# Moving places, splits and first loads around the low weights of a split-float32 encoder kernel

## The chip, the core and the metric

The kernel runs on one core of one Trainium2 chip. The metric is the device time of one execution in microseconds, lower is better. The engines are named as the profile names them: PE (TensorE, matmuls), PEld (its weight loads, which overlap the matmuls), DVE (VectorE), ACT (ScalarE), POOL (GpSimd) and SP (SyncE, which here issues most DMAs; SPq in a row is its queue).

## What is computed

One layer of a streaming encoder on 1024 prompt frames and 64 sample frames (1088 rows), all in float32: an input projection, a gated convolution, chunk-band attention, a gated merge, an output projection, and a SwiGLU feed-forward of width 2816.

```python
proj = xn @ w_in                    # cb, cc, ch, q, k, v, ga, gb
cv, conv_state = causal_conv(cc * ch, conv_prefix, w_conv)
ya = (cb * cv) @ w_conv_out
o, new_k, new_v = attn_fn(heads(q), heads(k), heads(v))
yb = o.reshape(B, L, ATT_DIM) @ w_attn_out
merged = jax.nn.sigmoid(ga) * ya + jax.nn.sigmoid(gb) * yb
x = x + merged @ w_out
x = x + (jax.nn.silu(xn2 @ w1) * (xn2 @ w3)) @ w2      # xn2 = rmsnorm(x)
return rmsnorm(x, g_final), conv_state, new_k, new_v
```

## The kernel before

**Split products.** A float32 operand is split in two float32r parts: ACT casts the high part, DVE subtracts it from the source to get the low part (`split`, lines 126 to 130). A product is then three matmuls, high by high, low rows by high weights, and high rows by low weights.

**Units.** The big projections go in units of 256 weight columns, 1024 deep, against all 1088 rows. A unit does seven block products (`STEPS`, a Strassen form of a 2 by 2 block product), each of 24 matmuls of 128x272. `Unit.prep(step)` makes the weights of one product; `run` issues a unit's products and, after each, calls `prep` of the next unit (`ahead`, a list of units and of the steps to be done at each turn). There are twelve units of the input projection (q, k and so on), then gates, attention, the merge, the output projection `wo`, and 22 units of the feed-forward's way up, named a0, b0, a1 ... b10 (a: `w_ff1`, b: `w_ff3`). The way down follows, in four blocks of two or three pairs of h columns, each block in two halves (g) of seven products.

**Places of the low weights.** High weights live in `ws`, eight buffers that rotate. Low weights live in one tile, `low`, in eight places of 512 columns: `slots` adds one to `taken` and takes the place `taken % 8`. Users put a shift on top: 0 for units, 40 for the merge's weights, 24 for `wo` (where the part in `low` is the high one), and 8 for the down products' h tiles (`h_load`, lines 1374 to 1390, which puts every second h tile in `ws` and the others in `low`). A shifted use of a place therefore reaches into the first columns of the next place; the framework that places the semaphores sees such an overlap and orders the two uses.

**First loads of the way down.** `refill` issues h loads as long as `held` plus the next group stays within 16 tiles; a group of the first block has two tiles. `held` starts at 14, so the first call (line 1527, before the last unit's products) loads group 0; `Refill.prep`, called after each product of b10, takes 2 off and loads the next group. SP issues DMAs in its program's order and waits there for each one's semaphores.

**Order.** The framework lists each engine's instructions by its own plan; `tc.issue_after(x)` pins what is issued within it behind instruction x. In `ahead` the entry `{2: (0, 1, 2)}` of the third unit makes steps 0, 1 and 2 after product 2, but after product 1 it falls back on step 1 as well, so that step 1 is split twice, in the projection's third unit (k0) and in the feed-forward's (a1).

**k tiles.** In the projections, small tiles share one scratch tile, `scr`, by lists of places: `KF` for a k result of 544 columns, `CC` and `STAGE` for others, with overlaps between them. The attention cache's tiles (`cache_tile`) use `CC`, in the order 4896, 5988, 9264, and are stored by DMA before a place can be used again.

Of the kernel before, what the change touches and what calls it, by code (L numbers as in the profile page):

```python
# [66 lines left out]
def encoder_kernel(ctx: ExitStack, tc: tile.TileContext, ins, outs):  # L67
# [49 lines left out]
    def table_load(j, t):  # L117

        t = tables[j] = t.rearrange("p (h n) -> p h n", h=2)
        src = ins["bias_ext"][2 * j, 384:]  # L120
        nc.sync.dma_start(t, bass.AP(tensor=src.tensor, offset=src.offset, ap=[[0, P], [768, 2], [1, 384]]))

    def table_store(j):
        nc.sync.dma_start(bias_d[2 * j : 2 * j + 2].rearrange("h (p n) -> p h n", n=384), tables.pop(j))
# [17 lines left out]
    taken = [-1]  # L142
# [55 lines left out]
    def temp():  # L198
        temps[0] += 1
        return temps[1][:, temps[0] % 2]  # L200

    class Unit:
        def __init__(self, src, nm):
            self.nm = nm
            self.raw = rpool.tile([P, KD, 2 * P], F32, tag="raw", name=f"raw{nm}")
            nc.sync.dma_start(self.raw, src.rearrange("(k p) n -> p k n", p=P))
            self.w = {}
# [8 lines left out]
        def prep(self, step):  # L216

            a11, a12, a21, a22 = self.block(0, 0), self.block(0, 1), self.block(1, 0), self.block(1, 1)

            def sum(o, x, y, op=ALU.subtract):  # L220
                vec.tensor_tensor(o, x, y, op=op)

            if step == 0:
                self.plain(1, a11)
            elif step == 1:
                self.plain(2, a12)
            elif step == 2:
                self.s1 = temp().rearrange("p (k n) -> p k n", k=4)
                sum(self.s1, a21, a22, ALU.add)
                self.s2 = temp().rearrange("p (k n) -> p k n", k=4)  # L230
                sum(self.s2, self.s1, a11)
                self.plain(6, self.s2)
            elif step == 3:
                sum(a21, a11, a21)
                self.plain(7, a21)
            elif step == 4:
                self.plain(5, self.s1)
            elif step == 5:
                self.plain(4, a22)
            else:  # L240
                sum(a12, a12, self.s2)
                self.plain(3, a12)

    newest = [None, None]
# [49 lines left out]
    def plain_load(i):  # L294
        ld, kt, at = plan[i]
        if "raw" not in ld:
            raw = rpool.tile([P, kt, ld["w"]], F32, tag="raw", name=f"rawp{i}")
            nc.sync.dma_start(raw, ld["src"].rearrange("(k p) n -> p k n", p=P))
            ld["raw"] = raw
# [58 lines left out]
    X, GM, SUMS, KEPT, VST, SQ, FEW = (0, 1024, 9264), 2048, 3072, (4096, 5120), (6144, 7168), 8192, 9216  # L358
    V32 = [10288]
    SNAP, STAGE, CC, UT = [544 * i for i in range(4)], [2720, 3808, 9264], [4896, 5988], [7080, 8172]  # L360
    KF = [*CC, 2176]
    turn = {tuple(KF): 0}

    def slot(places, n):

        k = turn[tuple(places)] = turn.get(tuple(places), -1) + 1
        a = places[k % len(places)]
        return scr[:, a : a + n]
# [164 lines left out]
    def unit_of(n):  # L533
        nm, u, src = units[n]
        return Unit(src, f"{nm}{u}")
# [35 lines left out]
    def whole(t, src, snap):  # L571

        two = t.rearrange("p (j n) -> p j n", j=2)
        if snap is None:
            act.copy(two, src)
        else:
            vec.tensor_tensor(two, src, snap, op=ALU.add)
# [53 lines left out]
    def k_done(u):  # L631
        def f(r, h, src, snap):
            kf = slot(KF, HT)
            whole(kf, src, snap)
            st = stage()
            split(st[:, 0], st[:, 1], kf)
            to_heads(k_d, st, 2 * u + r, h)
            late.append(lambda: k_out(2 * u + r, h, kf))
# [76 lines left out]
    def cache_load(i):  # L715
        cts[i] = ct = slot(UT, 2 * ATT)
        nc.gpsimd.dma_start(ct[:, :ATT], ck[i * P : (i + 1) * P])
        nc.gpsimd.dma_start(ct[:, ATT:], cvv[i * P : (i + 1) * P])

    def cache_tile(i):  # L720
        ct = cts[i]
        with tc.issue_after(newest[1]):
            put_v(slot(CC, 2 * ATT), ct[:, ATT:], P, TP + i * P, nc.sync)
        pk = bank1("BD", f"ckp{i}")[:, 0]
        for hp in range(4):
            nc.tensor.transpose(pk[:, hp * P : (hp + 1) * P], ct[:, hp * P : (hp + 1) * P], ident)
        st = slot(CC, 2 * ATT).bitcast(F32R).rearrange("p (l a t) -> p l a t", l=2, a=4)
        split(st[:, 0], st[:, 1], pk.rearrange("p (a t) -> p a t", a=4))
        dst = k_d[:, :, :, T + i * P : T + (i + 1) * P].rearrange("(a j) d l t -> (j d) l a t", j=2)
        for l in range(2):  # L730
            nc.sync.dma_start(dst[:, l], st[:, l].bitcast(F32))
# [9 lines left out]
    def run1(n, unit, ahead):  # L741
        nm, u, _ = units[n]
        return run(unit, x7, bank1, snap1, DONE[nm](u), ahead)
# [4 lines left out]
    ahead = []  # L748
# [7 lines left out]
    for n in range(len(units)):  # L756
        if n in (5, 6):
            for j in range(2):
                table_store(2 * (n - 5) + j)
        if n in (4, 5):  # L760
            for j in range(2):
                table_load(2 * (n - 4) + j, slot(STAGE, 768))
        if n == 0:
            r, si = r0, 2
        else:
            if n + 1 < len(units):
                nxt_unit = unit_of(n + 1)
                new = [(nxt_unit, {2: (0, 1, 2)} if n == 1 else {})]
            else:
                new = [(PlainNext(), {})]  # L770
                plain_load(0)
            if n == 1:
                ahead += new
                r, si = r1, 2
            else:
                r, si = run1(n, unit, new), 0
            unit = nxt_unit
        for _ in r:
            if n < 2 and si in (2 + n, 5 + n):
                i = 2 * n + si // 5  # L780
                cache_tile(i)
                if i + 2 < 4:
                    cache_load(i + 2)
            if si > 1:
                for f in due:
                    f()
                due.clear()
            due += late
            late.clear()
            si += 1  # L790
# [326 lines left out]
    def wo_half(hf):  # L1117
        r = []
        for kq in range(2):
            raw = rpool.tile([P, 4, 512], F32, tag="raw", name=f"wor{hf}_{kq}")  # L1120
            nc.sync.dma_start(
                raw,
                ins["w_out"][0][kq * 512 : (kq + 1) * 512, hf * 512 : (hf + 1) * 512].rearrange(
                    "(k p) n -> p k n", p=P
                ),
            )
            for k in range(4):
                hi, lo = moving_pair(f"o{hf}_{kq}_{k}")
                split(hi, lo, raw[:, k])
                r.append((hi, lo))  # L1130
        return r
# [34 lines left out]
    if True:  # L1166
# [2 lines left out]
        act.activation(gb_row, gb_row, AF.Copy, scale=-0.5)  # L1169

        two_sums = early.tile([P, 2, D], F32, tag="raw", name="two_sums")
        w = wo_half(0)
        for i in ORDER:
            t0, n = TT[i]
# [214 lines left out]
            ht.append(t)  # L1389
        hts.append(ht)  # L1390

    held = [14]

    def refill():

        while len(hts) < len(loads_h) and held[0] + len(loads_h[len(hts)][0]) <= 16:
            held[0] += len(loads_h[len(hts)][0])
            h_load(*loads_h[len(hts)])

    class Refill:  # L1400
        def prep(self, step):
            held[0] -= 2
            refill()

    class Down:
# [73 lines left out]
    def up_unit(n):  # L1479
        l, p = names[n]  # L1480
        return Unit(ins["w_ff1" if l == "a" else "w_ff3"][0][:, 2 * p * P : 2 * (p + 1) * P], f"{l}{p}")
# [3 lines left out]
        return run(unit, operands, bank2, snap2, (gate_done if l == "a" else hidden_done)(p), ahead)  # L1485


    u0, u1 = up_unit(0), up_unit(1)
    u0.prep(0)
    u0.prep(1)  # L1490
# [28 lines left out]
    for n in range(1, len(names)):  # L1519
        if n + 1 < len(names):  # L1520
            unit = up_unit(n + 1)
            ahead = [(unit, {2: (0, 1, 2)} if n == 1 else {})]
        else:
            for kp in (*blocks[0], blocks[1][0]):
                W2[kp] = Down(kp)
            ahead = [(W2[kp], {}) for kp in blocks[0]] + [(Refill(), {})]
            refill()
        if n in (4, 6):
            nm, src = (("k", ck), ("v", cvv))[n // 2 - 2]
            with tc.issue_after(stored[0]):  # L1530
                nc.gpsimd.dma_start(outs[f"cache_{nm}_sample"][: CACHE - TS], src[TS:])
        if n == 1:
            nxt += ahead
            r = r1
        else:
            r = up_run(n, this, ahead)
        for _ in r:
            for f in kept_now:
                f()
            kept_now[:] = last_keep  # L1540
            last_keep.clear()
        this = unit
# [173 lines left out]
```

## Time and profile before

| what | value |
|---|---|
| time, median of 3 runs | 1515.86 us (1514.68 to 1515.95) |
| the profiled execution | 1516.27 us, span of the profile 1514.2 us |
| PE busy | 1475.1 us, 97% of the span |
| DVE busy | 981.1 us, 65% |
| ACT busy | 679.3 us, 45% |
| DMA | 264.72 MB, mean 175 GB/s |

By stretches of the span (us; the bounds are chosen by hand):

| stretch | what runs | PE busy of | granted PE clock |
|---|---|---|---|
| 0 to 70 | norm, v | 66.12 of 70 | 1.00 |
| 70 to 161 | q and k units | 89.86 of 91 | 1.00 |
| 320 to 600 | gates and attention | 278.46 of 280 | 1.00 |
| 645 to 760 | end of the merge, wo | 114.13 of 115 | 1.00 |
| 800 to 860 | up units begin | 58.19 of 60 | 1.00 |
| 860 to 1150 | up units | 289.68 of 290 | 1.00 |
| 1209 to 1275 | last up unit | 46.24 of 66 | 0.74 |
| 1275 to 1325 | way down begins | 50.00 of 50 | 1.00 |
| 1480 to 1514 | end | 26.34 of 34 | 0.93 |

A row of the timeline reads: start, duration, engine, line of the kernel, operation, output and inputs, shapes, count, and in brackets the engine's idle time just before it and what ended it. A row of the table of waits reads: who waited, for whom, then us in total, how many times, and the longest. A row of a table of windows gives the window, its length, each engine's busy time and count, the granted PE clock (1.00 is full), the DMA engines' share and GB/s.

### The profile page before, as it was taken

The page shows a single profiled execution, that of the slowest core. Times are in us where ns is not written, and L with a number is a line of the kernel's source. Part 1 is how long each engine was busy: PE and PEld are TensorE (multiplying, and loading weights), DVE is VectorE, ACT ScalarE, POOL GpSimd, SP SyncE. Part 2 cuts the span into 40 slices and gives each one's busy share as a digit, 9 for nine tenths or more (in the row PEclk, how much of TensorE's full clock was granted, in tenths as well). Part 3 has the DMA queues.
Part 4 walks back from the last instruction along what each step waited for, and adds up shares of the span by engine and source line. Part 5 has one row for each costly group of instructions (what it writes and reads, how often), then busy time and mean ns, then how long its engine had stood idle before and what let it go on. Part 6 is the DMA issues. An engine that isn't in the chain of part 4 may idle for free.

```text
span 1514.2 us, 26487 instructions
## 1 busy us (share of the span) xinstructions
PE 1475.1 (97%) x10200; PEld 1382.5 (91%) x10200; DVE 981.1 (65%) x1852; ACT 679.3 (45%) x1398; POOL 133.1 (9%) x243
## 2 busy tenths in 40 slices
PE   8999999999999999999999999999999967999997
PEld 6899999999989999998888999999999966888886
DVE  7975565725767646661798666667677635857577
ACT  7654333425767635430456444444444423513123
POOL 1400010001111110001000001010111100000000
PEclk9999999999999999999999999999999977999999
DMA  8685623287766468434424444444434434776675
GB/s 285 188 272 195 199 86 115 46 251 215 200 171 177 114 197 285 153 96 144 150 71 159 154 148 157 157 153 147 157 132 154 147 118 164 271 247 229 224 266 202
DMA packets 164029, 264.72 MB, mean 175 GB/s; under 512 B 18624, under 2 KB 98688, under 8 KB 163872
## 3 DMA queue, kind: packets, MB, share of 16 engines
q1 hardware_dynamic: 143040, 196.13, 41.3%
q0 software_dynamic: 19712, 64.81, 11.8%
q10 hardware_dynamic: 1152, 2.10, 0.4%
q8 instruction: 80, 1.31, 0.4%
q14 instruction: 45, 0.37, 0.1%
HBM read 172.89 MB, written 91.92 MB: 175 GB/s over the span
## 4 chain that ended last, share of the span: by engine, by line
PE 70%; issue 16%; DVE 5%; DMA 4%; ACT 2%; POOL 2%; SPq 1%; POOLq 0%; ACTq 0%; DVEq 0%
PE A L1629 8%; PE D L1629 4%; PE Ab L266 4%; PE Aa L266 3%; PE g L330 2%; PE g L331 2%; PE g L332 2%; PE B L1629 2%; PE wo L1139 2%; PE wo L1141 2%; PE wo L1140 2%; PE t L952 2%; PE Db L266 2%; PE pv L977 2%; DMA low<-h_d 2%
## 5 line engine op out<-in xcount | busy, mean ns | idle before, releaser
L330 PE MATMUL g<-xn,wp 128*128 128x272 f32 x384 | 112.7, 293 | 0.0
L331 PE MATMUL g<-xn,wp 128*128 128x272 f32 x384 | 111.6, 291 | 0.0
L332 PE MATMUL g<-xn,low 128*128 128x272 f32 x384 | 110.6, 288 | 0.0
L128 ACT CAST ring<-w2r 128x512 fp32r<-128x512 f32 (+1 forms) x78 | 42.6, 587 | 109.4 <-PE A L1629 50.3
L128 ACT CAST hq<-sa 128x512 fp32r<-128x512 f32 x73 | 45.2, 619 | 82.3 <-DVE sa L1334 54.6
L1318 POOL DMA_DIRECT2D h_d<-hq x73 | 38.9, 533 | 433.5 <-DVE hq L129 234.9
L863 DVE CUSTOM_DVE_ANT_0 p<-s,bb 128x640 f32<-128x640 f32 (+5 forms) x72 | 47.5, 661 | 42.4 <-DMA qd<-q_d 27.1
L330 PEld LDWEIGHTS g<-xn,wp 128*128 128x128 f32 x384 | 72.3, 188 | 0.9
L332 PEld LDWEIGHTS g<-xn,low 128*128 128x128 f32 x384 | 72.3, 188 | 0.5
L331 PEld LDWEIGHTS g<-xn,wp 128*128 128x128 f32 x384 | 72.3, 188 | 0.1
L1629 PE MATMUL A<-ring,low 128*128 128x512 f32 x264 | 72.4, 389 | 0.0
L1629 PE MATMUL A<-ring,ht 128*128 128x512 f32 x264 | 72.2, 389 | 0.0
L129 DVE TENSOR_TENSOR hq<-sa,hq 128x512 fp32r<-128x512 f32 x73 | 50.4, 691 | 29.8 <-ACT hq L128 29.6
L266 PE MATMUL Ab<-tt,wb 128*128 128x272 f32 x352 | 60.9, 296 | 2.7 <-ACT sb_Q L254 2.0
L129 DVE TENSOR_TENSOR low<-rawa,wa 128x512 fp32r<-128x512 f32 x56 | 38.4, 688 | 38.8 <-ACT wa L128 38.8
L129 DVE TENSOR_TENSOR ring<-w2r,ring 128x512 fp32r<-128x512 f32 (+1 forms) x78 | 48.9, 648 | 22.4 <-ACT ring L128 22.4
L266 PE MATMUL Ab<-mg,wb 128*128 128x272 f32 x352 | 60.9, 296 | 0.8 <-DVE sb L1329 0.8
L266 PE MATMUL Aa<-tt,wa 128*128 128x272 f32 x352 | 58.2, 287 | 1.7 <-ACT sa_Q L254 1.6
L1629 PEld LDWEIGHTS A<-ring,low 128*128 128x128 f32 x264 | 49.6, 188 | 10.3
L1629 PEld LDWEIGHTS A<-ring,ht 128*128 128x128 f32 x264 | 49.5, 188 | 10.3
L266 PE MATMUL Aa<-mg,wa 128*128 128x272 f32 x352 | 57.8, 286 | 0.5 <-DVE sa L1299 0.5
L128 ACT CAST wa<-rawa 128x512 fp32r<-128x512 f32 x56 | 34.6, 620 | 51.7 <-PE Ab L266 33.7
(543 smaller groups left out, 4511.9 us busy)
## 6 DMA issues: line engine op xcount, KB each, us to landing
h_d<-hq POOLq DMA_DIRECT2D x73, 512.0 KB, 3.4
ht<-h_d SPq DMA_DIRECT2D x77, 256.0 KB, 3.5
low<-h_d SPq DMA_DIRECT2D x77, 256.0 KB, 3.5
rawa<-in_w_ff SPq DMA_DIRECT2D x11, 1024.0 KB, 5.9
rawb<-in_w_ff SPq DMA_DIRECT2D x11, 1024.0 KB, 5.3
w2r<-in_w_ff SPq DMA_DIRECT2D x11, 1024.0 KB, 7.2
qd<-q_d SPq DMA_DIRECT2D x32, 272.0 KB, 4.5
rawp<-in_w_in SPq DMA_DIRECT2D x6, 1024.0 KB, 6.5
```

The costliest lines, as they stand in the source:

```text
L128: a = act.copy(hi, src)
L129: b = vec.tensor_tensor(lo, src, hi.bitcast(F32), op=ALU.subtract)
L266: newest[0] = mm(t[:, j, :HN], w[:, k, :], x[p][:, k, l, j * HN : (j + 1) * HN], start=p in (1, 2, 7) and k == 0 and n == 0, stop=k == 3 a ...
L330: mm(out, a, first, start=k == 0, stop=False)
L331: mm(out, a, then, start=False, stop=False)
L332: mm(out, b, p, start=False, stop=k == kt - 1)
L863: vec.tensor_tensor_reduce(out=s if len(ps.shape) == 2 else s.rearrange("p (a b) -> p a b", a=2), in0=ps, in1=bias if len(ps.shape) == 2 e ...
L952: nc.tensor.transpose(tp[:, i * P : (i + 1) * P], s[:, i * P : (i + 1) * P], ident)
L977: mm(pv[:, :, lo:hi], v[:, kb, :], pt[:, :, kb - base, lo:hi], start=i == 0, stop=i == len(blocks) - 1,)
L1139: mm(ps, x(k, 0), wh, start=f, stop=False)
L1318: stored[0] = nc.gpsimd.dma_start(h_d[p, c - 1], hq.rearrange("p i l t -> p (i l t)").bitcast(F32)).ins
L1629: mm(t, ht[k][:, j, x], w[:, l], start=p in (1, 2, 7) and k == 0 and n == 0, stop=k == len(ks) - 1 and n == 2, skip_group_check=p in (6, 5 ...
```

## The change

There are five edits. The k tiles' places become 4896, 2176, 5988 in that order, from the first. The third unit's step 1 is split once, in both stages, and in the feed-forward its splits are pinned behind the newest snapshot copy of PE's results on ACT (`newest[1]`). Ahead of `wo` one place of `low` is skipped. The way down's `held` starts at 16, the early call of `refill` is gone, and the last `Refill.prep` takes 4 off instead of 2, so that each group is issued one product later in the program and the last turn issues two.

```diff
-    KF = [*CC, 2176]
-    turn = {tuple(KF): 0}
+    KF = [CC[0], 2176, CC[1]]
+    turn = {}
...
-                new = [(nxt_unit, {2: (0, 1, 2)} if n == 1 else {})]
+                new = [(nxt_unit, {1: (), 2: (0, 1, 2)} if n == 1 else {})]
...
         two_sums = early.tile([P, 2, D], F32, tag="raw", name="two_sums")
+        taken[0] += 1
         w = wo_half(0)
...
-    held = [14]
+    held = [16]
...
     class Refill:
         def prep(self, step):
-            held[0] -= 2
+            held[0] -= 2 if step < 6 else 4
             refill()
...
+    class Behind:
+        def __init__(self, unit):
+            self.unit = unit
+
+        def prep(self, step):
+            with tc.issue_after(newest[1]):
+                self.unit.prep(step)
...
-            ahead = [(unit, {2: (0, 1, 2)} if n == 1 else {})]
+            ahead = [(Behind(unit), {1: (), 2: (0, 1, 2)})] if n == 1 else [(unit, {})]
         else:
...
             ahead = [(W2[kp], {}) for kp in blocks[0]] + [(Refill(), {})]
-            refill()
```

The count of places moves with it. Up to b10 the kernel before takes 8 places for v, 85 for the twelve units (one of them the double split), 40 for the gates and the merge, 16 for `wo` and 148 for 21 up units (again one double): 297, so b10 begins at place 297 mod 8 = 1. The changed kernel takes 8 + 84 + 40 + 1 + 16 + 147 = 296 and b10 begins at place 0. With the shift of 8, group n of the h loads writes, in the kernel before, the columns 512n + 8 to 512n + 520, of which the last eight are the first low weights of b10's product n. In the changed kernel group 0 writes 3592 to 4104, where b10 has nothing, and group n from 1 on writes over product n - 1 and the first eight columns of product n.

PE, the beginning of b10 (Ab, Bb and Db are PSUM tiles of its products, wb_1, wb_2, wb_7 high weights, low the low ones; what an instruction waits for stands in brackets). The kernel before:

```order
L266 MATMUL Ab_13872<-mg_6860,wb_1_13677 128x272 x3
L266 MATMUL Bb_13907<-mg_6861,wb_2_13708 128x272 [waits PE_49]
L266 MATMUL Bb_13907<-mg_6861,wb_2_13708 128x272 x3
L266 MATMUL Db_13984<-tt_8099,wb_7_13770 128x272 [waits DVE_49]
L266 MATMUL Db_13984<-tt_8099,wb_7_13770 128x272 x3
L266 MATMUL Ab_13872<-mg_6860,low 128x272 [waits DMAHW5_49]
L266 MATMUL Ab_13872<-mg_6860,low 128x272
```

The changed kernel, from the same place:

```order
L266 MATMUL Ab_13863<-mg_6857,wb_1_13671 128x272 x3
L266 MATMUL Ab_13863<-mg_6857,low 128x272 x2
L266 MATMUL Ab_13863<-mg_6857,wb_1_13671 128x272 x4
L266 MATMUL Ab_13863<-mg_6857,low 128x272 x2
L266 MATMUL Ab_13863<-mg_6857,wb_1_13671 128x272 x4
```

Before, the first low matmul of each of the seven products waits for a DMA (the load of the h tile that shares eight columns with it), and the high matmuls of the next products were drawn ahead of it. In the change no matmul of b10 waits for a DMA and the products stand one after the other.

ACT, the beginning of the feed-forward (sb_Q is the copy of a PE result that frees the PSUM tile Ab for b0's next product; wa are a1's high weights, cast from the raw weights rawa). The kernel before:

```order
L1303 ACTIVATE sa_10_9209<-sa_10_9209 128x544
L128 CAST wa_2_9247<-rawa_9245 128x512
L128 CAST wa_1_9276<-rawa_9245 128x512
L1297 ACTIVATE sa_01_9239<-Aa_8904 128x544
L128 CAST wa_2_9279<-rawa_9245 128x512
L128 CAST wa_6_9284<-sf_8893 128x512
L254 COPY sb_Q<-Ab_8995 128x544
```

The changed kernel:

```order
L1304 ACTIVATE sa_10_9206<-sa_10_9206 128x544
L1298 ACTIVATE sa_01_9236<-Aa_8901 128x544
L254 COPY sb_Q<-Ab_8992 128x544
L128 CAST wa_1_9270<-rawa_9242 128x512
L128 CAST wa_2_9273<-rawa_9242 128x512
```

Five instructions stood between the activation and sb_Q, four of them casts of a1's weights; now the copy stands ahead of all of a1's casts, of which there is one less.

DVE, the first k result (scr from Bk) in the k unit. The kernel before, then the changed one:

```order
L577 TENSOR_TENSOR scr<-Bk_1270,scr 128x544 [waits DMAHW7_49,DMAHW2_49]
L577 TENSOR_TENSOR scr<-Ak_1241,scr 128x544 [waits PE_49,Activation_49]
L577 TENSOR_TENSOR scr<-Dk_1336,scr 128x544 [waits DMAHW5_49,PE_49]
```

```order
L577 TENSOR_TENSOR scr<-Bk_1267,scr 128x544 [waits DMAHW5_49,PE_49,Activation_49]
L577 TENSOR_TENSOR scr<-Ak_1238,scr 128x544 [waits PE_49,Activation_49]
L577 TENSOR_TENSOR scr<-Dk_1333,scr 128x544 [waits DMAHW7_49,DMAHW2_49,PE_49]
```

The wait for the cache's last two k stores (DMAHW7 and DMAHW2, line 731, which read place 5988) moves from the first k result to the third, and the wait for the cache's last v store (DMAHW5, line 377, which reads place 4896) from the third to the first.

At `wo` the cast of its first high weights moves from a place whose columns overlap those of the merge's last weights to one that doesn't, so six of `wo`'s first eight splits stand ahead of the merge's last instructions on DVE instead of behind them.

## Prediction

> **What bounds the kernel now.** I began with the page: PE is busy for 97% of the span, so time can come only from its idle stretches or from the speed of its matmuls.
>
> ```profile
> span 1514.2 us, 26487 instructions
> PE 1475.1 (97%) x10200; PEld 1382.5 (91%) x10200; DVE 981.1 (65%) x1852; ACT 679.3 (45%) x1398; POOL 133.1 (9%) x243
> PEclk9999999999999999999999999999999977999999
> ```
>
> 39 us are idle, and in slices 33 and 34 of 40 (1211 to 1287 us) the granted clock is not full. The table of waits, for PE alone, says which waits these are:
>
> ```profile
> PE Ab L266 <- DMA low<-h_d: 12.0, 4, 3.4
> PE Db L266 <- DMA low<-h_d: 3.4, 2, 2.3
> PE Ab L266 <- ACT sb_Q L254: 2.0, 2, 1.3
> PE Bb L266 <- DMA low<-h_d: 1.3, 1, 1.3
> PE ktp L624 <- DVE scr L577: 1.1, 1, 1.1
> PE wo L1143 <- ACT low L128: 0.8, 1, 0.8
> ```
>
> Seven waits, 12.0 + 3.4 + 1.3 = 16.7 us, are for the way down's h loads into `low`. All are in the last up unit, b10. The timeline gives its first instruction, its first wait, its last instruction and the way down's first:
>
> ```profile
> 1218.34 0.66 PE L266 MATMUL Ab<-mg,wb 128*128 128x272 f32 x4
> 1223.34 0.82 PE L266 MATMUL Ab<-mg,low 128*128 128x272 f32 x2 [3.33 <-DMA low<-h_d]
> 1274.00 0.41 PE L266 MATMUL Ab<-mg,low 128*128 128x272 f32 x2
> 1274.24 0.85 PE L1629 MATMUL A<-ring,ht 128*128 128x512 f32 x3
> ```
>
> So b10 lasts 1274.24 - 1218.34 = 55.90 us. The table of windows sets it beside an undisturbed unit (first row), parts of b10 that follow a wait, and the way down (last two rows):
>
> ```profile
> 1176.90:1197.62 20.72, 20.72 (x170) 20.72 (x169) 12.65 (x21) 7.93 (x17) 1.06 (x2) 1.00 0.27 96
> 1218.34:1274.24 55.90, 36.19 (x170) 33.29 (x169) 18.31 (x31) 11.73 (x23) 1.59 (x3) 0.69 0.34 119
> 1223.30:1228.50 5.20, 4.90 (x20) 4.58 (x20) 0.20 (x1) 0.22 (x1) 0.00 (x0) 0.50 0.00 0
> 1247.70:1250.60 2.90, 2.75 (x20) 2.53 (x20) 0.00 (x0) 0.06 (x1) 0.00 (x0) 1.00 0.00 0
> 1253.90:1258.80 4.90, 4.90 (x20) 4.58 (x20) 0.00 (x0) 0.00 (x0) 0.00 (x0) 0.50 0.01 3
> 1275.00:1325.00 50.00, 50.00 (x224) 41.48 (x223) 41.15 (x70) 26.87 (x53) 2.67 (x5) 1.00 0.79 276
> 1325.00:1480.00 155.00, 155.00 (x695) 128.67 (x694) 104.06 (x178) 36.54 (x71) 0.00 (x0) 1.00 0.72 241
> ```
>
> The same work takes 20.72 us in a unit and 55.90 in b10. Of the difference, 55.90 - 36.19 = 19.7 us is idle (the seven waits and 3.0 us more for drains), and 36.19 - 20.72 = 15.5 us is matmuls at a low clock: twenty matmuls take 4.90 us at 0.50 and 2.75 at 1.00. From 1275 to 1480 PE never idles: that stage sets its own length, and follows wherever b10 ends.
>
> **Part by part: the low places and the first loads.** By the order, b10's matmuls wait for no DMA any more. What they still wait for are the drains of PSUM on ACT and DVE, as in every unit. If these are in time, b10 takes 20.72 us and ends at 1218.34 + 20.72 = 1239.06: **35.2 us** less. The drains share their engines with the splits for the way down, which had 55.90 us before. Is 20.72 enough? On DVE the first of that work waits for a weight load, and the rate is seen where DVE runs without a gap:
>
> ```profile
> 1216.94 0.37 SPq L1411 DMA_DIRECT2D w2r<-in_w_ff  x1
> 1222.08 0.69 DVE L1426 TENSOR_TENSOR w2r<-w2r 128x512 f32<-128x512 f32 x1 [5.17 <-DMA w2r<-in_w_ff]
> 1278.21 0.69 DVE L1321 TENSOR_TENSOR sa<-sa,sa 128x512 f32<-128x512 f32 x1
> 1278.82 0.69 DVE L129 TENSOR_TENSOR ring<-sa,ring 128x512 fp32r<-128x512 f32 x1
> 1274.93 0.84 PE L1629 MATMUL A<-ring,low 128*128 128x512 f32 x3
> ```
>
> On DVE, start to start is 0.61 us. SP issues that weight load at 1216.94, before b10 begins, so its landing doesn't move. In the changed order 31 DVE instructions go from this one to the product on b10's last PSUM tile that the way down's second product waits for; two of them are short. By 29 x 0.61 + 0.2 = 17.9 us DVE is there at 1240.0 us; PE needs it at 1239.06 plus the first product of 12 matmuls. Three of those start every 0.68 us (1274.93 follows 1274.24 by 0.69), 2.7 us in all, so at 1241.8: 1.8 us to spare. The drain that b10's last product needs (start 1239.06 - 2.96 = 1236.1) is the 20th: 1222.08 + 19 x 0.61 + 0.1 = 1233.8, or right after product 4 at 1233.1 + 0.7; the way down's first product needs the 25th by 1239.06, at 1236.9. ACT has 11.73 us of work in the whole of b10. So I take the full 35.2; should the cover fail, the ends are 19.7 (idle gone, clock not) and 35.2.
>
> The loads themselves: group n is issued when b10's product n has begun to read its low weights, every 2.96 us (a seventh of 20.72) from 1221 on, the last at 1239, and used at 1239 + 2.7n and later. Group 1, issued at 1222, is needed at 1241.8. They land within
>
> ```profile
> DMA to landing us min/median/max: 2.9/4.2/11.3
> w2r<-in_w_ff SPq DMA_DIRECT2D x11, 1024.0 KB, 7.2
> ```
>
> (the second row, the median of the kind of weight load above, is for a rival), so even the longest, 11.3 us, is hidden: 0. The extra SP waits on PE hold only loads that are used later: 0.
>
> **The k tiles.** The first k result waited for the cache's last k store (issued at 116.35), and PE waited for the result:
>
> ```profile
> 117.50 0.41 PE L266 MATMUL Bk<-xn,low 128*128 128x272 f32 x2
> 121.15 0.72 DVE L577 TENSOR_TENSOR scr<-Bk,scr 128x544 f32<-128x544 f32 x1 [2.10 <-DMA k_d<-scr]
> 131.22 0.73 DVE L577 TENSOR_TENSOR scr<-Dk,scr 128x544 f32<-128x544 f32 x1 [0.69 <-PE Dk L266]
> 122.02 0.27 PE L624 MATMUL ktp<-ident,scr 128*32 128x128 f32 x1 [1.14 <-DVE scr L577]
> 111.44 0.36 SPq L377 DMA_DIRECT2D v_d<-scr  x1
> 116.35 1.07 SPq L731 DMA_DIRECT2D k_d<-scr  x1
> 104.65 3.62 DMA v_d<-scr
> ```
>
> Now it waits for the v store of 111.44. An earlier one took 3.62 us, so this is there at 115.1, before the matmuls end (117.9). The result is ready at about 118.7, two microseconds before PE wants it (120.9). The wait for the k store moves to the third result, whose matmuls end at 131.2, ten after the landing at 121.1. **1.1 us** (ends: 0 and 1.1).
>
> **The feed-forward's third unit.** ACT's casts of a1 waited for its raw weights, and the copy that PE needed stood behind them:
>
> ```profile
> 810.61 1.14 ACT L128 CAST wa<-rawa 128x512 fp32r<-128x512 f32 x2 [4.32 <-DMA rawa<-in_w_ff]
> 813.78 0.61 ACT L254 COPY sb_Q<-Ab 128x544 f32<-128x544 f32 x1
> 814.44 0.77 PE L266 MATMUL Ab<-tt,wb 128*128 128x272 f32 x4 [1.34 <-ACT sb_Q L254]
> 809.72 0.41 PE L266 MATMUL Ab<-tt,low 128*128 128x272 f32 x2
> ```
>
> The copy now stands ahead and can start when its matmuls end, at 810.1; PE wants it at 814.44 - 1.34 = 813.1. **1.3 us** (ends 0 and 1.3). Late next would be a1's own splits, but a1 begins only after a further unit has run. The two double splits that go (an ACT cast and a DVE subtraction of the 0.69-us kind each) ran beside PE: 0 further.
>
> **wo.** PE's 0.8 us for the cast ends, since that cast no longer waits for the merge's last matmul.
>
> ```profile
> 671.86 0.29 PE L332 MATMUL yb<-ob,low 128*128 128x272 f32 x1
> 674.19 0.19 DVE L129 TENSOR_TENSOR ms<-ga,ms 128x32 fp32r<-128x32 f32 x1
> ```
>
> In return wo's first tile is not interleaved with the second and needs DVE's last merge rows after 14 matmuls, 3.2 us into it at 0.23 us each (a third of the 0.69 above, the same shape); before, these rows were done 2.3 us after the merge's end (674.38 against 672.15). **0.8 us** (ends 0 and 0.8; a loss would need DVE 0.9 us later).
>
> **Sum.** 35.2 + 1.1 + 1.3 + 0.8 = 38.4 us off the profiled span of 1514.2: 1475.8. That execution took 1516.27, 0.41 above the median of the runs, 1515.86; off the median the forecast is **1477.4 us**.
>
> [...] The row 1223.30:1228.50 shows 0.50 right behind a gap of 3.33 us, and 1253.90:1258.80 too. [...] The trace sides with the gaps as the cause: 20.72-us units at 1.00 stand ahead, and the way down at 1.00 behind.
>
> **Rivals.** *The clock stays low in b10.* If something other than the waits lowers it (both quoted stretches at 0.50 last 5 us, longer than the gap ahead), the idle time goes, the 15.5 us stay: 1477.4 + 15.5 = 1492.9. Against it: it is 1.00 in all other units, with the same matmuls.
>
> *DVE becomes the bound at the end of b10.* If the weight load lands at 7.2 us after issue (the median of its kind on the page) instead of some 5, and DVE paces at 0.69, the 31 instructions end at 1224.1 + 20.2 = 1244.3, 2.5 us late; with a clock drop behind it, up to 5: 1480 to 1482.5. For it: DVE has hardly a gap left there. Against: the way down kept DVE at 41 of 50 us without a PE wait.
>
> *The waits move to the way down: slower.* If the loads, now issued behind the products of a short b10, are not ahead of PE, each product of the way down's first block pays what b10's paid, 35.2 / 7 = 5.0 us. From 8 products on (38.4 / 5.0) the change loses; all fourteen would give 1477.4 + 70 = 1547. Against it: 11.3 us at worst to land, with 17 and more to go, and PE at 50.00 of 50 while the same loads run.
>
> *The change doesn't take the waits away.* Then only the three small terms are left: 1515.86 - 3.2 = 1512.7. The order of the built program speaks against it.
>
> **How the numbers follow.** Forecast 0.83, DVE bound 0.10, clock 0.03, moved waits 0.02, waits kept 0.02. The likeliest gives 1477.4. The range starts 2 us below it, since no more waits than these end, and goes past the DVE case to 1484; outside are about 0.1. What can be told from no change is 0.2%, 3 us: faster 0.97, within 0.01, slower 0.02.
>
> **What would show it.** In the new profile b10 should run about 20.7 us at clock 1.00, without a row of PE waiting for low<-h_d, and the waits for ktp, sb_Q (the longer one) and wo's cast be gone; PE idle falls from 39 to about 16 us. A PE wait at L1637 or L1472 in the first 10 us of the way down would mean the DVE rival. I am wrong if b10 stays above 25 us, or if the way down grows by more than it shrinks.

## The result, and the profile after

| | before | after |
|---|---|---|
| median of four runs | 1515.9 us | 1475.53 us |
| lowest and highest | 1514.68, 1517.61 | 1475.21, 1479.49 |
| span of the profiled execution | 1514.2 us | 1473.8 us |

The ratio of the times is 0.9739, 95% interval 0.9720 to 0.9758: 40 us faster. The forecast was 1477.4. In some executions below, a stretch of the up units or of the way down runs 1.8% slower at a granted clock of 1.00 (321 matmuls instead of 327 in 40 us), so stages are compared there, not whole times.

The head of the changed kernel's page, and of its table of waits for PE the only rows of 0.6 us and more:

```profile
span 1473.8 us, 26481 instructions
PE 1458.0 (99%) x10200; PEld 1369.7 (93%) x10200; DVE 979.2 (66%) x1850; ACT 678.1 (46%) x1396; POOL 133.1 (9%) x243
PEclk9999999999999999999999999999999999999999
```

```profile
PE warm L443 <- ACT ones L441: 2.9, 1, 2.9
PE Aa L266 <- ACT sa_Q L254: 1.3, 1, 1.3
PE pvv L512 <- ACT low L128: 0.9, 1, 0.9
PE xt L1212 <- DVE xg L1201: 0.6, 1, 0.6
```

PE's idle time is 15.8 us instead of 39, the granted clock has no slice of the page below 0.9 left, and no row of PE waits for `low<-h_d`, for `ktp`, for `sb_Q` or at `wo`. Then b10 and the way down in windows (us; busy time of PE, PEld, DVE, ACT and POOL, granted clock, DMA share, GB/s), and the timeline where the one ends and the other begins, with DVE's first and last work for it:

```profile
1213.13:1233.85 20.72, 20.72 (x171) 20.72 (x170) 16.82 (x28) 11.37 (x22) 1.06 (x2) 1.00 0.82 264
1235.00:1285.00 50.00, 50.00 (x224) 41.48 (x223) 41.92 (x72) 26.66 (x52) 3.21 (x6) 1.00 0.81 292
```

```profile
1216.71 0.69 DVE L1427 TENSOR_TENSOR w2r<-w2r 128x512 f32<-128x512 f32 x1 [5.02 <-DMA w2r<-in_w_ff]
1233.85 0.85 PE L1637 MATMUL A<-ring,ht 128*128 128x512 f32 x3
1234.66 0.71 DVE L1328 TENSOR_TENSOR sa<-Ab,sa 128x544 f32<-128x544 f32 x1
1236.57 0.84 PE L1637 MATMUL B<-ring,ht 128*128 128x512 f32 x3
```

b10 takes 20.72 us, an undisturbed unit's time to the hundredth, where it took 55.90. The way down behind it fills its 50.00 us of 50 as before. From its first matmul to the end of the span it is 1473.8 - 1233.85 = 239.95 us, before 1514.2 - 1274.24 = 239.96: nothing is given back later. DVE was done with b10's last tile at 1235.37, and PE came for the tile at 1236.57, so 1.2 us were to spare.

**Where the 40.4 us come from.** Each row compares the start of the same PE instruction in both traces; the change of that lead from row to row is what a place gave.

| place | start before | start after | lead | given there |
|---|---|---|---|---|
| k unit, last product ahead of `ktp` | 117.75 | 117.90 | -0.15 | |
| k unit, behind the first `ktp` | 122.04 | 120.89 | 1.15 | 1.30 |
| k unit, behind the last `ktp` | 148.52 | 147.82 | 0.70 | -0.45 |
| merge (yb) | 587.98 | 587.07 | 0.91 | 0.21 |
| up units, behind `wo` | 796.96 | 794.59 | 2.37 | 1.46 |
| b0, behind `sb_Q` | 817.52 | 813.53 | 3.99 | 1.62 |
| b10 begins | 1218.34 | 1213.13 | 5.21 | 1.22 |
| way down begins | 1274.24 | 1233.85 | 40.39 | 35.18 |

The loss of 0.45 us is a wait that the new places of the k tiles brought; the page does not list it under PE, since it shows only on the weight load. The changed kernel's timeline there:

```profile
144.39 0.41 ACT L625 COPY scr<-ktp 32x128 f32<-32x128 f32 x2 [0.31 <-PE Ak L266]
144.70 0.55 PEld L266 LDWEIGHTS Dk<-xs,wk 128*128 128x128 f32 x4 [0.36 <-ACT scr L625]
```

ACT's small copy of a `ktp` result, done in time before, now waits for a matmul, and the next product's weight load waits for the copy. To the 0.21 us up to the merge no run assigns a cause; the 1.22 us between b0 and b10 have a section below.

### The profile page after: what moved, and what is told of

Same layout as the page of the kernel before. It is cut to its first block, busy times and chain, and to the rows that moved or that the text cites. A ratio compares the mean times of both kernels' runs of the same rounds, so it can differ in the third digit from the quotient of the medians.

```text
span 1473.8 us, 26481 instructions
## 1 busy us (share of the span) xinstructions
PE 1458.0 (99%) x10200; PEld 1369.7 (93%) x10200; DVE 979.2 (66%) x1850; ACT 678.1 (46%) x1396; POOL 133.1 (9%) x243
## 4 chain that ended last, share of the span: by engine, by line
PE 92%; DVE 3%; DMA 2%; ACT 1%; SPq 1%; issue 1%; ACTq 0%; DVEq 0%
PE Ab L266 9%; PE Aa L266 8%; PE A L1637 8%; PE Db L266 4%; PE Da L266 4%; PE D L1637 4%; PE g L330 2%; PE g L331 2%; PE g L332 2%; PE B L1637 2%; PE Bb L266 2%; PE Ba L266 2%; PE wo L1139 2%; PE wo L1141 2%; PE wo L1140 2%; PE t L952 2%
## 5 line engine op out<-in xcount | busy, mean ns | idle before, releaser
L266 PE MATMUL Ab<-tt,wb 128*128 128x272 f32 x352 | 57.8, 285 | 0.0
```

What stands on the lines that cost most here:

```text
L266: newest[0] = mm(t[:, j, :HN], w[:, k, :], x[p][:, k, l, j * HN : (j + 1) * HN], start=p in (1, 2, 7) and k == 0 and n == 0, stop=k == 3 a ...
```

## Experiments: what made b10 long

Theory: a product of b10 waits because the load of an h group, which writes the first eight columns of the product's low weights, stands ahead of the product's reads; the load itself waits for the product before, so each product pays a transfer. In the kernel before, b10's second product starts its last matmuls at 1235.81; SP then issues the next load, and PE goes on when it has landed:

```profile
1236.46 0.37 SPq L1386 DMA_DIRECT2D low<-h_d  x1
1239.74 0.82 PE L266 MATMUL Ab<-tt,low 128*128 128x272 f32 x2 [3.44 <-DMA low<-h_d]
```

Rivals: loads during b10 cost by themselves; or the place at which b10 begins is what counts.

**The first loads alone.**

```diff
-    held = [14]
+    held = [16]
...
-            held[0] -= 2
+            held[0] -= 2 if step < 6 else 4
...
-            refill()
```

> The kernel before with the edit of the first loads alone (held from 16, no early call, 4 off at the last turn); b10 still begins at place 1. Theory 'order of read and load': a product waits because the load of group n stands ahead of product n's reads and shares eight columns with them; later loads alone end all seven waits: 1515.9 - 35.2 = 1480.7 us, b10 20.7 us, no PE row waiting for low<-h_d. Rival 'both edits are needed' (the place b10 begins at matters too): some of the seven waits stay, at 5.0 us each, 1485.7 us or more. Rival 'place alone': 1515.9.

**No shift, loads as early as before.**

```diff
-                a = taken[0] % 8 * 512 + 8
+                a = taken[0] % 8 * 512
```

> The kernel before with the shift of the h tiles' places 0 in place of 8, so that group n writes only the place of product n - 1; loads as early as before. Theory 'order of read and load' (eight shared columns): the waits end, 1515.9 - 35.2 = 1480.7 us. Rival 'early loads are what costs' (256 KB transfers during b10, whatever their columns): they are issued as early as before, so 1515.9, b10 near 56 us.

b10 in windows, the first loads alone, then no shift:

```profile
1219.09:1239.81 20.72, 20.72 (x171) 20.72 (x169) 16.82 (x28) 11.37 (x22) 1.06 (x2) 1.00 0.80 267
```

```profile
1218.14:1238.86 20.72, 20.72 (x170) 20.72 (x169) 16.81 (x28) 11.37 (x22) 1.07 (x2) 1.00 0.79 271
```

Both give 20.72 us at clock 1.00, with no DMA wait of PE. The times are 1478.91 us (ratio 0.9767, 0.9739 to 0.9795) and 1485.2 us (0.9806, 0.9777 to 0.9835). The second is above the forecast for another reason: its way down took 244.0 us instead of 240.0, with no wait of PE for another engine or a DMA (177 matmuls in 40 us instead of 180, at 1.00), and its wait for `ktp` was 2.0 us. So either of these two edits by itself ends all seven waits: loads during b10 cost nothing in these two runs, where they share no columns with a product still to come, and the place of b10 need not change.

**The place alone.**

```diff
         two_sums = early.tile([P, 2, D], F32, tag="raw", name="two_sums")
+        taken[0] += 1
```

> The kernel before with one place of low skipped ahead of wo, alone; b10 begins at place 2, loads early as before. Theory 'order of read and load': group n still shares columns with product n, except where the place wraps round from 7 to 0 (one of seven products): six waits stay, 1515.9 - 5.0 - 1.5 (wo: PE's offset against the changed kernel grows from 0.91 to 2.37 there) = 1509.4 us. Rival 'place alone': 1479. Rival 'nothing but wo': 1514.4.

Measured: 1504.92 us (0.993, 0.9908 to 0.9953). b10 in the table of windows, and its DMA waits:

```profile
1216.11:1260.91 44.80, 29.16 (x170) 26.82 (x168) 15.70 (x27) 10.63 (x21) 1.07 (x2) 0.81 0.36 125
```

```profile
PE Ab L266 <- DMA low<-h_d: 8.4, 3, 3.2
PE Db L266 <- DMA low<-h_d: 2.0, 1, 2.0
PE Bb L266 <- DMA low<-h_d: 2.0, 1, 2.0
```

b10 is still 44.80 us with five waits in the trace, so the place alone does not end them. But two waits went, not one. The last product has no shared columns here, and PE took its matmuls while the load for the product before it landed. That covered the sixth wait.

**One and four waits.** The shift is 0 for the first groups and 8 from group 6, or from group 3, on. In both kernels the way down is changed too: a later load then writes over eight columns of an h tile that is still to be read, so only b10 is compared.

```diff
-                a = taken[0] % 8 * 512 + 8
+                a = taken[0] % 8 * 512 + (8 if loaded[0] >= 12 else 0)
```

> The kernel before with the shift 0 for groups 0 to 5 and 8 from group 6 on, so that only b10's last product shares columns with its load: one wait instead of seven. 'Each wait pays its own gap and its own clock drop': 1480.7 + 35.2 / 7 = 1485.7 us, with matmuls at 0.50 behind the gap. [...]

> The kernel before with the shift 0 for groups 0 to 2 and 8 from group 3 on: the last four of b10's products share columns with their loads. 'Each wait pays its own gap and clock drop': 1480.7 + 4 x 5.0 = 1500.8 us. 'The clock falls once and stays low until the last wait is over': four gaps at up to 3.3 us and three to four products of 2.96 us at half speed, 1480.7 + 13.2 + 11.8 = 1505.7 us or less by as much as gaps are shorter. 'Gaps alone': 1493.9.

b10 with one wait, then with four (in the second kernel the bound is 6 instead of 12), each in the table of windows and then its DMA waits:

```profile
1222.76:1249.87 27.11, 22.77 (x170) 22.55 (x169) 17.89 (x31) 11.74 (x23) 1.60 (x3) 0.94 0.71 245
```

```profile
PE Ab L266 <- DMA low<-h_d: 4.3, 1, 4.3
```

```profile
1217.39:1257.85 40.46, 30.24 (x170) 28.51 (x169) 18.02 (x31) 11.64 (x23) 1.59 (x3) 0.75 0.46 164
```

```profile
PE Ab L266 <- DMA low<-h_d: 5.3, 2, 3.4
PE Db L266 <- DMA low<-h_d: 2.8, 2, 1.7
```

One wait costs 27.11 - 20.72 = 6.4 us, of which 4.3 are the gap; four cost 19.7, or 4.9 each; seven cost 35.2, or 5.0 each. With one wait the clock is 0.50 for 3.4 us (the last row of the last section's windows). Not every gap is followed by 0.50. In the kernel before it follows the first gap of b10, 3.33 us long (the prediction's row 1223.30:1228.50); with the place alone the first gap, 3.17 us, leaves the clock at 1.00 (last section).

With four waits the total does not tell the first two expectations apart, since with the gaps as measured (8.1 us) the second one gives 19.9. The matmuls do: four of them take 1.11 us at 1231.93, 0.66 at 1233.22 and 1.11 again at 1238.18, behind the second wait. So the clock comes back between waits; it does not stay low until the last one. Whole times, 1497.89 and 1506.7 us, hold the way down's own waits and do not tell.

## Experiments: the small terms

**The k tiles' places as before**, in the changed kernel:

> The changed kernel with the k tiles' places as before (4896, 5988, 2176, starting from the second). Theory: PE's wait for the first k result, 1.1 to 1.3 us, is back at ktp, and the wait of 0.36 us that the changed order has behind the last ktp (for ACT's copy) goes: about 0.9 us longer, 1476.4. Rival 'hidden anyway' (the time is lost again by the end of the k units): the same as the changed kernel, 1475.5.

1477.22 us; the wait for `ktp` is back (1.6 us), and the lead lost is 1.79 us there and 1.32 behind the last `ktp`; the span is 1.4 us longer. So the edit is worth 1.32 us against this kernel, and 1.30 - 0.45 = 0.85 by the table of leads; the wait that it ends was 1.62 us here and 1.14 there. The rival (hidden anyway) is out.

**The skipped place behind `wo`** instead of ahead of it:

> The changed kernel with the skipped place behind wo in place of ahead of it, so that wo's places are as the double split's loss leaves them and b10's as in the change. wo's places are then shifted by one against the kernel before, so the cast of wo's first weights may or may not overlap the merge's last weights. Theory 'an overlap at wo costs 1.5 us': with an overlap 1477.0 us and PE waiting at wo for ACT's cast, without one 1475.5. Rival 'the interleaving costs, not the place': the offset at wo stays as in the changed kernel.

1478.99 us. PE's waits in `wo` (45 us around it) are back as before:

```profile
PE wo L1143 <- ACT low L128: 0.8, 1, 0.8
PEld wo L1144 <- DVE wo L129: 0.5, 1, 0.5
```

Against the changed kernel it falls from 0.06 us behind ahead of `wo` to 1.50 behind it: 1.44 us lost, as much as the change gave there. The overlap costs PE the cast's 0.8 and then a weight load's 0.5 for the split's second half. The interleaved order of `wo`'s matmuls came back with the overlap, so the two are not parted; the waits are for the cast and the split. The rest of the 3.5 us between the two spans came later, 1.8 of it between b0 and b10, where PE waits 1.5 us for `sa_Q` (see below).

**The third unit.** First the pin alone undone, twice, then the whole edit:

```diff
-            ahead = [(Behind(unit), {1: (), 2: (0, 1, 2)})] if n == 1 else [(unit, {})]
+            ahead = [(unit, {1: (), 2: (0, 1, 2)})] if n == 1 else [(unit, {})]
```

> The changed kernel with the splits of the feed-forward's third unit not pinned (still once each). Theory: ACT's casts of a1 stand ahead of the copy sb_Q again and wait for raw weights; PE waits 1.3 us more, 1.6 with the restart: 1477.1 us. Rival 'the double split was the cause, not the order': 1475.5. Besides, three short waits for sa_Q later in the way up (1.2 us in all), which the changed kernel does not have: if they hang on the pin they are back (1478.3), if on chance or the places they are not.

> The changed kernel without the pin once more. 'The copy's wait hangs on when the raw weights land': PE's wait for sb_Q goes with the landing, anywhere from 0 to 1.3 us (0.3 in the first run). 'It is the double split': 0.3 or less again. The later waits for sa_Q, 2.9 us in the first run: less here if they are chance, the same if the pin ended them.

> The changed kernel with the feed-forward's third unit as before: step 1 split twice, nothing pinned (b10 then begins at place 1). My step 'PE waits 1.3 us because the copy sb_Q stands behind a1's casts, which wait for raw weights': the wait is back at sb_Q, between 0.3 us (raw weights landing as early as in the run without the pin) and 1.3 us (as late as before). Rival 'the wait hangs on the double split, not on when the raw weights land': 1.3 us, while the kernel without the pin alone stays at 0.3.

ACT's first cast of a1 and PE's product behind `sb_Q`: no pin, no pin again, and the double split:

```profile
806.27 1.14 ACT L128 CAST wa<-rawa 128x512 fp32r<-128x512 f32 x2 [2.63 <-DMA rawa<-in_w_ff]
810.72 0.78 PE L266 MATMUL Ab<-tt,wb 128*128 128x272 f32 x4 [0.27 <-ACT sb_Q L254]
```

```profile
805.50 1.14 ACT L128 CAST wa<-rawa 128x512 fp32r<-128x512 f32 x2 [1.65 <-DMA rawa<-in_w_ff]
810.50 0.66 PE L266 MATMUL Ab<-tt,wb 128*128 128x272 f32 x4
```

```profile
807.16 1.14 ACT L128 CAST wa<-rawa 128x512 fp32r<-128x512 f32 x2 [3.79 <-DMA rawa<-in_w_ff]
810.98 0.77 PE L266 MATMUL Ab<-tt,wb 128*128 128x272 f32 x4 [0.80 <-ACT sb_Q L254]
```

Taken against the instant at which PE would have gone on (its start less its wait), the raw weights came 5.0 us ahead (no wait), 4.2 us ahead (0.27), 3.0 us ahead (0.80) and, in the kernel before, 2.5 us ahead (1.34). So the wait follows the landing, with or without the double split, and the pin takes the copy out of its reach. That the double split adds anything of its own is not shown: with it there is one cast more ahead of the copy, and the two runs that have it are also the two with late landings. Times: 1478.94, 1476.88 and 1481.49 us; in the way up of the last one PE did 321 matmuls in 40 us instead of 327. The first run's profile holds later waits too: between b0 and b10 PE waits 2.5 us for `sa_Q` there, 0.7 in the second run's and never in the double split's, so it is not the pin that ends those.

**The 1.2 us that no edit aimed at.** Between b0 and b10 the kernel before waits three times for `sa_Q` (1.0 us on its weight loads, of which the matmuls' rows list one), the changed one never. Is that the change?

> The changed kernel once more, unaltered. The profile before has three short waits for sa_Q late in the way up (1.2 us in all) that the changed one lacks, and the stores of h ahead of them land later there. If that is chance of one execution, such waits may show here too, with late stores; if it comes from the change's places, there are none here, in any execution: span 1473.8 within 0.3.

It is not: the changed kernel can wait there too. Its second profile, on ACT and PE in unit a4, and behind it the same place in the first one:

```profile
951.76 0.62 ACT L128 CAST hq<-sa 128x512 fp32r<-128x512 f32 x1 [3.20 <-DMA h_d<-hq]
955.42 0.60 ACT L254 COPY sa_Q<-Aa 128x544 f32<-128x544 f32 x1
956.08 0.77 PE L266 MATMUL Aa<-tt,wa 128*128 128x272 f32 x4 [0.83 <-ACT sa_Q L254]
```

```profile
950.59 0.62 ACT L128 CAST hq<-sa 128x512 fp32r<-128x512 f32 x1 [1.52 <-DMA h_d<-hq]
954.26 0.60 ACT L254 COPY sa_Q<-Aa 128x544 f32<-128x544 f32 x1
```

ACT's cast waits for a store of h to free its buffer, 3.20 us in this execution and 1.52 in the first, and the copy behind it comes 1.16 us later, although PE was 0.67 us ahead of the first execution at b0. Where b10 begins it is 0.60 behind: 1.27 us lost, about what the kernel before lost. Over the other kernels that still split these tiles ahead of the copy, the same wait of the cast lies between 1.1 and 4.1 us. The second median was 1477.59 us, 2 above the first.

**A version without that wait.** Two of the seven h tiles of each pair are split and stored behind `sa_Q`:

```diff
-            keep(6, d)
             minus(b, b, d)
             if p == NF // 2 - 1:
+                keep(6, d)
+            else:
+                last_keep.append(lambda: keep(6, d))
...
-            for f in kept_now:
-                f()
-            kept_now[:] = last_keep
+            for f in [f for w, f in kept_now if w == 0]:
+                with tc.issue_after(newest[1]):
+                    f()
+            kept_now[:] = [(w - 1, f) for w, f in kept_now if w] + [(3, f) for f in last_keep]
```

> The changed kernel with two of each pair's seven h tiles (c = 6 and 3) split and stored behind the next unit's copy sa_Q instead of ahead of it. Theory 'sa_Q is late because a cast ahead of it on ACT waits for a store of h to free its buffer': no PE wait for sa_Q is left after 820 us, however late the stores land; 1475.5 less nothing to 1 us, and its slowest executions are nearer its fastest. Rival 'DVE or PSUM is what is late': the waits stay, or move to the next copy, and the time is 1475.5 or more.

```profile
952.02 0.62 ACT L128 CAST wb<-rawb 128x512 fp32r<-128x512 f32 x1 [0.60 <-PE Aa L266]
952.54 0.61 ACT L254 COPY sa_Q<-Aa 128x544 f32<-128x544 f32 x1
```

The cast ahead of the copy now waits for a product of PE's. No wait for a store is left on ACT in the way up, and none for `sa_Q` on PE. The four runs lie between 1475.09 and 1475.41 us, those of the unaltered change beside them on the same chip between 1475.73 and 1480.49. Against the kernel before it is 0.9733 (0.9709 to 0.9757), against the change within the intervals: steadier, but not shown to be faster than its best executions.

## Why the prediction was right, step by step

- *b10 35.2 us.* Measured 35.18, with both halves gone together: the idle 19.7 and the 15.5 of low clock. The clock rival (1492.9) fell with it.
- *Which edit does it.* The prediction took "the low places and the first loads" as one step. The runs part them: the first loads do all of it, the place alone leaves five of the seven waits.
- *DVE as the bound.* DVE began at 1216.71 (forecast, less the lead of 5.21: 1216.87) and ended 0.6 us later than forecast, with 1.2 us to spare instead of 1.8. No PE wait followed.
- *Waits that move to the way down.* None: PE is full there from its first matmul.
- *k tiles 1.1 us.* 1.30 at the place, 0.45 lost again at a later `ktp`, so 0.85 net (1.32 in the other pair of traces): the step named where the stall of the first result goes (the k store, to the third result), but not what ACT's copies would wait for.
- *Third unit 1.3 us.* 1.62: the mechanism as told, and 0.3 more, since the weight load waits for the copy too, 1.6 us where the matmul's row has 1.34. Its size hangs on one DMA's landing.
- *`wo` 0.8 us.* Mis-sized: 1.46, and 1.44 when the skipped place was moved. The table of waits had been read for PE alone; the weight load's row (0.5 us for DVE's half of the split) was part of the same stall.
- *Left out.* 1.22 us of waits for `sa_Q`, which come and go between executions of one kernel. The sum came out 2.0 us short of the profile's 40.4, mostly by this and by `wo`. The range began 2 us below the forecast "since no more waits than these end"; more did end, and 1475.53 lies 0.1 us above that bound. A second set of runs of the same kernel, 1477.59, lies on the forecast. The two sets differ by as much as the sum falls short, so how near either median lies is in part luck.

## What to carry to other kernels

When a tile is cut into places by a count and some users shift theirs by a few columns, a transfer can share columns with a place it has nothing to do with; look for a DMA's name in the waits of matmuls that do not use its data. Then ask of each early load what it must wait for and who must wait for it: here eight columns tied each load between two products, and issuing it one product later was enough. A stall on PE is to be read on PE and on its weight loads together, and a wait that ends with a DMA deserves a second execution before it is booked to an edit.

## What was not expected of the hardware

The clock does not follow the gaps by their length. In the kernel before, its eight changes in b10 (at 1222.3, 1236.0, 1239.4, 1242.8, 1253.0, 1266.7, 1270.1 and 1273.5) lie 3.41 us apart or a multiple of it. Three views of windows cut from a change in steps of that length (length, PE's busy time and count, granted clock, DMA share, GB/s): before; the place alone, with the end of its first gap; one wait.

```profile
1218.87:1222.29 3.42, 1.14 (x10) 1.00 1.01 394
1222.29:1225.70 3.41, 2.36 (x10) 0.50 0.09 35
1225.70:1229.11 3.41, 2.71 (x13) 0.50 0.07 16
1229.11:1232.53 3.42, 2.08 (x8) 0.50 0.54 176
1232.53:1235.94 3.41, 3.41 (x17) 0.50 0.00 0
1235.94:1239.35 3.41, 0.36 (x3) 1.00 0.56 188
1239.35:1242.76 3.41, 3.02 (x13) 0.50 0.38 153
1242.76:1246.18 3.42, 1.89 (x13) 1.00 0.40 105
1246.18:1249.59 3.41, 1.89 (x15) 1.00 0.26 91
```

```profile
1219.35:1222.76 3.41, 1.82 (x14) 1.00 0.28 105
1222.76:1226.18 3.42, 1.72 (x12) 1.00 0.46 145
1226.18:1229.59 3.41, 2.40 (x10) 0.50 0.13 47
```

```profile
1220.94 0.52 PE L266 MATMUL Ab<-mg,low 128*128 128x272 f32 x2 [3.17 <-DMA low<-h_d]
```

```profile
1239.85:1243.26 3.41, 1.66 (x14) 1.00 0.59 184
1243.26:1246.68 3.42, 0.83 (x6) 1.00 0.75 294
1246.68:1250.09 3.41, 3.41 (x17) 0.50 0.18 73
```

In these rows a window at full clock in which PE is busy for 1.14 us or less is followed by one at 0.50; one with 1.82 or 1.89 is not; of 1.66 and 1.72 the one is not and the other is. Windows at 0.50 with 2.08 to 2.71 us busy are followed by another at 0.50 where the next one is shown; in the kernel before those with 3.02 and 3.41 are followed by one at 1.00.

Two gaps later in the b10 of the kernel before:

```profile
1247.70 0.52 PE L266 MATMUL Db<-tt,low 128*128 128x272 f32 x2 [2.34 <-DMA low<-h_d]
1253.90 0.82 PE L266 MATMUL Ab<-tt,low 128*128 128x272 f32 x2 [1.93 <-DMA low<-h_d]
```

So the length of a gap alone does not tell: 3.17 us of idle left the clock at 1.00 with the place alone, as 2.34 us did in the kernel before, where the drop at 1253.0 fell in the gap of 1.93 us. With one wait the clock fell 0.8 us after PE had gone on. Nor was PE idle for the whole of the windows that ended in a drop: it was busy for 1.14 of 3.42 us in one (before) and for 1.72 of 3.42 in another (the place alone). What decides instead, no run here shows.
